# An RWKV-7 scan on one Trainium2 core: another interleaving of its steps, another order of one product, and sums over contiguous elements

## Chip, cores and metric
One core of a Trainium2 chip runs the whole program. The metric is the device time in microseconds, the median over the runs shown. The engines are named as in the profile: PE (TensorE matmul), PEld (its weight loads), DVE (VectorE), ACT (ScalarE), POOL (GpSimd) and SP (SyncE, which here issues DMAs).

## The reference, cut to what matters
Four layers on 256 latent and 256 context tokens of 1024 channels: attention, RWKV-7, pooling, attention, each followed by a squared-ReLU MLP. Only the RWKV layer's scan is touched. It runs per head (16 heads of 64), per direction, first over the context, then over the latent tokens:

```python
def step(state, inp):
    r_t, w_t, k_t, v_t, kk_t, a_t = inp
    sa = jnp.einsum("bhvk,bhk->bhv", state, kk_t)
    state = (state * w_t[:, :, None, :]
             - sa[..., None] * (kk_t * a_t)[:, :, None, :]
             + v_t[..., None] * k_t[:, :, None, :])
    return state, jnp.einsum("bhvk,bhk->bhv", state, r_t)
for d in range(N_DIRS):
    s_ctx, yc = _wkv_scan(zero, r_c, dec_c[d], key_c[d], v_c, kk_c, a_c[d], d == 1)
    _, yl = _wkv_scan(s_ctx, r_l, dec_l[d], key_l[d], v_l, kk_l, a_l[d], d == 1)
```
The output of a head is then normalised, a bonus is added, it is multiplied by a gate and projected.

## The kernel before, in words
Everything outside the scan is dense products in three matmuls of rounded parts (`mm3`, L261) and is not touched. The scan (`rwkv_scan`, L828) is written in chunks of 64 tokens. A **unit** is one pair of heads (`cc`, 8 of them) of one stream (`s`, context then latent), so there are 16 units, each with 2 directions (`dd`), 2 heads (`hh`) and 4 chunks (`q`). For a unit the kernel builds a 64 by 64 triangular matrix per chunk, inverts it, and turns the recurrence into products of 64 by 64 blocks.

The work on a unit is a set of Python generators; each `next` issues one **step**. A step is called here by its letter and number:
- **a1 to a4** (`front_a`, L920): a1 a broadcast product (L925) and DVE `kkn`; a2 eight decay products (L932) and four ACT Tanh; a3 DVE scaling and two running sums (L945), then ACT Exp `E` and `iL` and POOL `key`, `kkh`; a4 one DVE product (L960). In the order a1, a2 stand as `a`, a3, a4 as `A`.
- **b1 to b4** (`front_b`, L963): b1 four DVE and four POOL products into `KB`, `AR`; b2 and b3 sixteen PE instructions each (L978), two DVE products into `NG` (L983) and a DMA of `NG` to DRAM (`Ls`); b4 the DMA of the diagonal blocks back (`Nb`).
- **c1 to c6** (`front_c`, L990): POOL and DVE `ks`; transposes of `KB` (L1005), `AR` (L1011) and `v` (L1021) through PSUM, copied by ACT; c6 a head sum (L1028) and DVE L1029.
- **z1 to z5** (`base`, L1033): inversion of the 16 by 16 diagonal blocks on DVE, 64 blocks at once on 64 partitions. z1 to z3 eliminate inside 8 by 8 (L1049, L1051); z4 and z5 form the block off the diagonal as a product and a sum over the innermost axis of an 8 by 8 by 8 tensor (L1055 to L1059), then a transposed copy (L1060) and DMAs to DRAM (`Xs`) and back as `XT` and `X`.
- **l1 to l4** (`levels`, L1084): 16 to 32 to 64, products of 32 PE instructions (L1094) with DVE or ACT in between (L1106, L1108, L1114, L1116). **k** (`mv`, L1073): 32 more (L1078).
- **h1 to h5** (`chunks`, L1119): h1 and h2 products by the inverse (L1127), each followed by ACT copies `G` and `VU` (L1130, L1132); h3 the G products (L1137), read by DVE into `P` and `Rp` (L1143, L1144); h4 L1151; h5 L1160, read by DVE into `Q` (L1162).
- **x1 to x8** (`chain`, L1165): the state from chunk to chunk, alternately a product with DVE `S` (L1181, L1186) and an output product (L1191).
- **f1 to f3** (`finish_a`, L1196): ACT copy (L1200) and DVE add (L1201) of the output, two averages (L1204, L1208). **g** (`norms`, L1287), every fourth iteration (and one head pair at a time in the last ones): ACT table load, Ln and Exp (L1213, L1214); **G1 to G4** the DVE normalisation (L1222 to L1228), ACT and POOL (L1230, L1231); **G5, G6** the gates (L1235: PE L1237, L1238, DVE L1239, ACT L1241, DVE L1242).

The main loop (L1303) runs `n` from -4 to 15. In each turn, an **iteration**, it walks a string `STEPS`; a letter issues the next step of unit `n + AHEAD[letter]`, so units at different stages are interleaved:
```python
AHEAD = dict(l=1, k=1, x=0, z=2, c=2, f=0, h=1, b=3, a=4, g=0, G=-1, A=3, L=2)
```
From n = 0 on, PE and DVE must execute in exactly the order of the string (`ordered`, L78); ACT, POOL and the DMA queue are free to follow the framework's schedule. For n below 0 no order is forced.

PSUM has eight banks: `inv` 2, `chain` 1, `yps` 1, `pre` 2 (`pt(1)`), `lora` 1 (`pt(0)`) and `warm` 1. The last is written only by `warm`, which with `WARM = [{}]` issues none of its matmuls; it does call `later`, which places early r-projections (L883) before n = -1. SBUF tag `t1` has one buffer, shared by `kkh` and `vr`; `finish_a` works in `self.sqr`, which is also the scratch of the normalisation.

Of the kernel before, what the change touches and what calls it, by code (L numbers as in the profile page):

```python
# [6 lines left out]
F32 = mybir.dt.float32  # L7
# [13 lines left out]
class Kern:  # L21
# [806 lines left out]
    def rwkv_scan(self, R, W, U, ps, psu, K, V, Rr, hid, xr):  # L828
# [22 lines left out]
        self.it = 0  # L851
        wb = ps.tile([128, NT], F32, name="warm", tag="warm", bufs=1)
        busy = W.tile([128, T], F32R, name="busy")
        nc.scalar.copy(busy, hid["w"][:, 0:T])

# [32 lines left out]

        def warm(z):

            at = lambda plan: plan[min(self.it + 4, len(plan) - 1)].get(z, 0)
            for _ in range(at(WARM)):
                self.tc.keep_in_program_order(nc.tensor.matmul(wb[:, 0:T], lhsT=busy[:, 0:128], rhs=busy, start=True, stop=True))
            later(at(LATER))
        with self.pool("rwDram", 1, space=bass.MemoryType.DRAM) as dr:
# [21 lines left out]
            def pt(z=1):  # L917
                return ps.tile([128, NT], F32, name="pre", tag=("lora", "pre")[z], bufs=(1, 2)[z])

            def front_a(cc, s, w2, st):  # L920

                kc = K[cc]
                sl = slice(s * T, s * T + T)
                pk = pt(0)
                nc.tensor.matmul(pk[:, :T], lhsT=w2[32:64, 2], rhs=hid["kinv"][:, sl], start=True, stop=True)  # L925
                kkn = W.tile([128, T], F32, name="kkn")
                nc.vector.scalar_tensor_tensor(kkn, kc[:, sl], v["k_k"][:, cc:cc + 1], pk[:, :T], op0=ALU.mult, op1=ALU.mult)
                yield
                tw = W.tile([128, 2, T], F32, name="tw")
                ta = W.tile([128, 2, T], F32, name="ta")  # L930
                pz = [pt(dd) for dd in range(2)]
                self.in_turn([nc.tensor.matmul(pz[dd][:, z * T:z * T + T], lhsT=w2[rows(dd), z], rhs=hid[n][rows(dd), sl],  # L932
                                               start=True, stop=True) for z, n in enumerate("wa") for dd in range(2)])
                warm("a")
                for dd in range(2):
                    nc.scalar.activation(tw[:, dd], pz[dd][:, :T], AF.Tanh, bias=hb[:, dd, cc:cc + 1], scale=0.5)
                for dd in range(2):
                    nc.scalar.activation(ta[:, dd], pz[dd][:, T:], AF.Tanh, bias=hb[:, 2 + dd, cc:cc + 1], scale=0.5)
                yield

                cum = W.tile([128, 2, T], F32, name="cum")
                nc.vector.tensor_scalar(tw, tw, 1.0, -0.5 * DEC, op0=ALU.add, op1=ALU.mult)
                for dd in range(2):
                    src = tw[:, dd, ::-1] if dd else tw[:, dd]
                    nc.vector.tensor_tensor_scan(cum[:, dd], c["scanm"], src, 0.0, op0=ALU.mult, op1=ALU.add)  # L945
                E = W.tile([128, 2, 4, 65], F32, name="E")
                nc.gpsimd.memset(E[:, :, :, 0:1], 1.0)
                nc.scalar.activation(E[:, :, :, 1:65].rearrange("p d q t -> p (d q) t"),
                                     cum.rearrange("p d (q t) -> p (d q) t", q=4), AF.Exp)
                lam = W.tile([128, 2, 4], F32, name="lam", tag="lam", bufs=4)  # L950
                nc.gpsimd.tensor_copy(lam, E[:, :, :, 64])
                iL = W.tile([128, 2, T], F32, name="iL")
                nc.scalar.activation(iL, cum, AF.Exp, scale=-1.0)
                key = W.tile([128, 2, T], F32, name="key")
                nc.scalar.activation(key, ta, AF.Identity, scale=ka[:, 0, cc:cc + 1], bias=ka[:, 1, cc:cc + 1])
                nc.gpsimd.tensor_mul(key, key, kc[:, sl].unsqueeze(1).broadcast_to([128, 2, T]))
                kkh = W.tile([128, T], F32, name="kkh", tag="t1")
                nc.gpsimd.tensor_scalar_mul(kkh, kkn, 0.5)
                yield
                nc.vector.scalar_tensor_tensor(ta, ta, 1.0, kkh.unsqueeze(1).broadcast_to([128, 2, T]), op0=ALU.add, op1=ALU.mult)  # L960
                st.update(kkn=kkn, E=E, lam=lam, iL=iL, key=key, b=ta)

            def front_b(cc, s, st, it):  # L963
# [12 lines left out]
                for dd in range(2):  # L976
# [3 lines left out]
                                  for q in range(4) for hh in range(2)])  # L980
                    warm("b")
                    for hh in range(2):
# [7 lines left out]
            def front_c(cc, s, st):  # L990
# [10 lines left out]
                VU = U.tile([128, 2, 4, 2, 64], F32, name="VU", tag="VU", bufs=2)  # L1001
                for dd in range(2):
                    pn = pt().rearrange("p (q x) -> p q x", q=4)
                    for q in range(4):
                        nc.tensor.transpose(pn[:, q], flat(KB[:, dd, q]), c["ident"])  # L1005
                    warm("c")
                    nc.scalar.copy(NG[:, dd, :, :, 2], pn.rearrange("p q (h x) -> p h q x", h=2))
                    yield
                pn = pt().rearrange("p (q x) -> p q x", q=4)
                for q in range(4):  # L1010
                    nc.tensor.transpose(pn[:, q], flat(AR[:, q, 0]), c["ident"])  # L1011
                warm("d")
                nc.scalar.copy(XR[:, :, :, 0], pn.rearrange("p q (h x) -> p h q x", h=2))
                yield
                vr = W.tile([128, T], F32, name="vr", tag="t1")
# [6 lines left out]
                for dd in range(2):  # L1022
                    for par in range(2):
                        nc.scalar.copy(VU[rows(dd), dd, par::2].rearrange("p q h x -> p q (h x)"), pv[rows(par), dd])
                st.update(XR=XR, VU=VU)
                yield
                pb = pt()
# [5 lines left out]
            def base(st, it):  # L1033
# [10 lines left out]
                for j in range(7, 0, -1):  # L1044
# [6 lines left out]
                    nc.vector.tensor_sub(Z8[:, :, 0:j, j:8], Z8[:, :, 0:j, j:8], t)  # L1051
                yield
                by_row = lambda ap: ap.unsqueeze(2).broadcast_to([64, 8, 8, 8])
                by_col = lambda ap: ap.rearrange("p a b -> p b a").unsqueeze(1).broadcast_to([64, 8, 8, 8])
                nc.vector.tensor_mul(tm, by_row(N16[:, 0:8, 8:16]), by_col(Z[:, 8:16, 8:16]))  # L1055
                nc.vector.tensor_reduce(wt, tm, axis=mybir.AxisListType.X, op=ALU.add)
# [16 lines left out]
            def mv(st):  # L1073
# [3 lines left out]
                for dd, hh, q in units:  # L1077
                    nc.tensor.matmul(p[rows(g(dd)), hh, q], lhsT=NG[rows(dd), dd, hh, q, 0], rhs=VU[rows(dd), dd, q, hh],  # L1078
                                     start=True, stop=True)
                warm("k")  # L1080
                nc.scalar.copy(XR[:, :, :, 1], p)
                yield

            def levels(st):  # L1084
# [11 lines left out]
                for lv, m in enumerate((16, 32)):  # L1096
# [6 lines left out]
                    p = prod(L, of(X))  # L1103
                    warm("l")
                    if lv == 0:
# [5 lines left out]
                    if lv == 0:  # L1111
                        p2 = prod(of(XT), of(Tz))
                    warm("m")
                    nc.vector.tensor_sub(cols(XT, 1), cols(XT, 1), cols(p, 1))  # L1114
# [4 lines left out]
            def chunks(st):  # L1119
# [3 lines left out]
                for hh in range(2):  # L1123
                    p = psu.tile([128, 4, 2, 64], F32, name="inv", tag="inv", bufs=2)
                    for q in range(4):
                        for dd in range(2):
                            nc.tensor.matmul(flat(p[rows(g(dd)), q]), lhsT=XT[rows(g(dd)), hh, q],  # L1127
                                             rhs=flat(XR[rows(g(dd)), hh, q]), start=True, stop=True)
                    warm("h")
                    nc.scalar.copy(G1[:, hh], p[:, :, 0])  # L1130
                    for dd in range(2):
# [6 lines left out]
                                               rhs=flat(NG[rows(g(dd)), dd, hh, q, 1:3]), start=True, stop=True)  # L1138
                              for hh in range(2) for q in range(4) for dd in range(2)])
                warm("i")  # L1140
                for dd in range(2):
# [23 lines left out]
            def chain(st, s):  # L1165
                nonlocal S
                P, Rp, Q, yp, lam = [st[n] for n in ("P", "Rp", "Q", "yp", "lam")]
                for q in range(4):
# [7 lines left out]
                    if not (s == 0 and q == 3):  # L1176
                        bank = psu.tile([128, NT], F32, name="chain", tag="chain", bufs=1)
                        p = bank[:, 0:128].rearrange("p (d t) -> p d t", d=2)
                        for dd in range(2):
                            for hh in range(2):  # L1180
                                nc.tensor.matmul(p[rows(hh), dd], lhsT=P[rows(hh), dd, q], rhs=So[rows(hh), dd],  # L1181
                                                 start=True, stop=True)
                        warm("x")
                        S = U.tile([128, 2, 64], F32, name="S", tag="S", bufs=3)
# [11 lines left out]
            def finish_a(cc, s, yp, y2):  # L1196

                sl = slice(s * T, s * T + T)
                y = self.sqr[:, 0:T]
                nc.scalar.copy(y, yp[:, 0])  # L1200
# [33 lines left out]

            def gate(cc, w2, y):  # L1235
                pf = pt(0)
                nc.tensor.matmul(pf, lhsT=w2[:, 0], rhs=hid["g"][:, 0], start=True, stop=False)  # L1237
                nc.tensor.matmul(pf, lhsT=w2[0:32, 1], rhs=hid["g"][0:32, 1], start=False, stop=True)  # L1238
                nc.vector.tensor_mul(y, y, pf)  # L1239
                H, L = [R.tile([128, NT], F32R, name="kvr", tag="kvr", bufs=24) for _ in range(2)]  # L1240
# [46 lines left out]
            def norms(cc, s):  # L1287
# [9 lines left out]
                for c2, r in two:  # L1297
                    yield
                    gate(c2, w2s[c2][1], ycs[c2][0])
                yield  # L1300
# [36 lines left out]

AHEAD = dict(l=1, k=1, x=0, z=2, c=2, f=0, h=1, b=3, a=4, g=0, G=-1, A=3, L=2)
STEPS = [[(z, AHEAD[z]) for z in order.split()] for order in (
    "k l l l z z z z z c c c c c c h h h h h A A b b L b b a a",  # L1340
    "x x A l z x x A l z k z G l x x z G h z G h G x x c f G c G c b f c c c h f h h b L a b b a g")]

ORDERED = 0
IN_ORDER = (mybir.EngineType.PE, mybir.EngineType.DVE)

WARM = [{}]

# [158 lines left out]
```

## Time and profile before

| | us |
|---|---|
| median of 3 runs | 2518.07 |
| lowest, highest | 2516.51, 2520.76 |
| profiled execution | 2517.29 |
| its span, first to last instruction | 2515.5 |

On the page, PE is busy 93% of the span, DVE 68%, ACT 44%, POOL 13%; the granted TensorE clock of the execution is 0.963 of full speed. "PE busy" includes matmuls that wait in the array behind others. Times within the span count from its start; the scan lies between about 795 and 1345 us. An idle time in brackets behind an instruction is the engine's wait before it and what ended it. A group of matmuls is shown with the time from its first start to its last modelled end, so that the next group's start can lie before it.

### The profile page before, as it was taken

The numbers are of one execution on the slowest core, as the hardware profiler recorded it, in microseconds if no ns is written. First come the engines' busy times: TensorE is split into PE (matmuls) and PEld (weight loads), VectorE is DVE, ScalarE is ACT, GpSimd is POOL, SyncE is SP. The second block draws the span as 40 slices with busy tenths as digits, with TensorE's granted clock in tenths as the row PEclk, the third lists the DMA queues.
The fourth block names the chain that finished last, engine by engine and source line by source line (L and its number), as shares of the span: only waits on it lengthen the run. The fifth ranks groups of instructions, "written<-read, shape, count | busy, mean of one in ns | idle before, by whom it ended". The sixth has DMA issues, their size and how long they took to land.

```text
span 2515.5 us, 41677 instructions
## 1 busy us (share of the span) xinstructions
PE 2333.6 (93%) x16992; PEld 1890.5 (75%) x16992; DVE 1707.8 (68%) x2813; ACT 1102.4 (44%) x2015; POOL 325.2 (13%) x406
## 2 busy tenths in 40 slices
PE   7999999999799978878789999999999999988999
PEld 5556888888677767666667888888888888866999
DVE  5767787674786667666756777755787674787555
ACT  4678523323564334343434432323523323476443
POOL 0100001100201222222200100110001100010110
PEclk9999999999899998888989999999999999999999
DMA  7431354552123311212222355442254552203453
GB/s 279 182 112 34 126 200 175 194 200 105 69 81 98 90 37 36 40 37 37 41 60 97 118 184 214 170 168 89 80 201 170 198 199 86 73 26 109 168 185 135
DMA packets 154833, 308.32 MB, mean 123 GB/s; under 512 B 107153, under 2 KB 111633, under 8 KB 122769
## 3 DMA queue, kind: packets, MB, share of 16 engines
q1 hardware_dynamic: 154640, 305.65, 35.6%
q8 instruction: 134, 2.20, 0.4%
q14 instruction: 59, 0.48, 0.1%
HBM read 294.58 MB, written 11.03 MB: 121 GB/s over the span
## 4 chain that ended last, share of the span: by engine, by line
PE 77%; DVE 10%; ACT 5%; DMA 4%; issue 3%; POOL 1%; SPq 0%; DVEq 0%; POOLq 0%; ACTq 0%
PE mm L261 52%; PE mm L272 3%; PE po L631 2%; PE pre L261 2%; PE inv L1127 2%; DMA Nb<-Ls 1%; DMA Ls<-NG 1%; PE pre L978 1%; PE pt L626 1%; DVE wL L251 1%; PE sc L615 1%; PE rps L883 1%; ACT wH L250 1%; DVE Zb L1051 1%; PE inv L1094 1%
## 5 line engine op out<-in xcount | busy, mean ns | idle before, releaser
L251 DVE TENSOR_TENSOR wL<-wraw,wH 128x1024 fp32r<-128x1024 f32 (+1 forms) x364 | 412.1, 1135 | 268.6 <-ACT wH L250 267.7
L250 ACT CAST wH<-wraw 128x1024 fp32r<-128x1024 f32 (+1 forms) x364 | 341.9, 943 | 449.2 <-PE mm L261 430.2
L261 PE MATMUL mm<-hH,wH 128*128 128x512 f32 (+1 forms) x1296 | 471.4, 364 | 3.9 <-ACT wH L250 3.9
L261 PE MATMUL mm<-hH,wL 128*128 128x512 f32 (+1 forms) x1296 | 471.8, 364 | 1.9 <-DVE wL L251 1.8
L261 PE MATMUL mm<-hL,wH 128*128 128x512 f32 (+1 forms) x1296 | 466.6, 360 | 0.0
L261 PE MATMUL mm<-uH,wH 128*128 128x512 f32 (+1 forms) x1072 | 380.6, 355 | 0.0
L261 PE MATMUL mm<-uL,wH 128*128 128x512 f32 (+1 forms) x1072 | 379.4, 355 | 0.3
L261 PE MATMUL mm<-uH,wL 128*128 128x512 f32 (+1 forms) x1072 | 379.5, 354 | 0.0
L201 DVE SCALAR_TENSOR_TENSOR acc<-wraw,sc_sb,acc 128x2048 f32<-128x2048 f32 x126 | 302.8, 2419 | 47.9 <-DMA wraw<-in_w_mod 42.8
L392 POOL TENSOR_TENSOR usq<-relu 128x512 f32<-128x512 f32 (+1 forms) x128 | 144.8, 1132 | 1248.3 <-ACT relu L390 1248.3
L261 PEld LDWEIGHTS mm<-hH,wH 128*128 128x128 f32 x1296 | 245.5, 189 | 57.5 <-ACT wH L250 13.2
L261 PEld LDWEIGHTS mm<-hH,wL 128*128 128x128 f32 x1296 | 245.7, 190 | 42.1 <-DVE wL L251 4.4
L261 PEld LDWEIGHTS mm<-hL,wH 128*128 128x128 f32 x1296 | 245.8, 190 | 35.9 <-issue 0.2
L261 PEld LDWEIGHTS mm<-uL,wH 128*128 128x128 f32 x1072 | 202.3, 189 | 29.3 <-DVE uL L396 1.1
L261 PEld LDWEIGHTS mm<-uH,wH 128*128 128x128 f32 x1072 | 202.6, 189 | 28.3
L261 PEld LDWEIGHTS mm<-uH,wL 128*128 128x128 f32 x1072 | 202.6, 189 | 28.2
L339 DVE SCALAR_TENSOR_TENSOR x<-mm,mod,x 128x256 f32<-128x256 f32 x272 | 122.0, 479 | 133.7 <-PE mm L261 133.4
L390 ACT ACTIVATE relu<-mm 128x512 f32<-128x512 f32 (+1 forms) x128 | 69.2, 544 | 295.6 <-PE mm L261 282.8
L272 PE MATMUL mm<-hH,wH 128*128 128x256 f32 (+1 forms) x232 | 76.4, 331 | 25.9 <-ACT hH L322 14.5
L395 ACT CAST uH<-usq 128x512 fp32r<-128x512 f32 (+1 forms) x128 | 72.7, 569 | 46.4 <-POOL usq L392 46.4
L1127 PE MATMUL inv<-XR,XT 64*64 64x128 f32 x512 | 52.0, 383 | 36.7 <-DVE XT L1114 36.7
L396 DVE TENSOR_TENSOR uL<-usq,uH 128x512 fp32r<-128x512 f32 (+1 forms) x128 | 80.5, 630 | 5.6 <-ACT uH L395 4.8
(340 smaller groups left out, 3734.6 us busy)
## 6 DMA issues: line engine op xcount, KB each, us to landing
wraw<-in_w_mod SPq DMA_DIRECT2D x96, 1024.0 KB, 4.8
wraw<-in_w_in SPq DMA_DIRECT2D x64, 1024.0 KB, 6.0
wraw<-in_w_out SPq DMA_DIRECT2D x64, 1024.0 KB, 5.4
wraw<-in_w_qk SPq DMA_DIRECT2D x10, 1024.0 KB, 4.8
wraw<-in_w_rkv SPq DMA_DIRECT2D x9, 1024.0 KB, 4.8
wraw<-in_w_ao SPq DMA_DIRECT2D x16, 512.0 KB, 4.0
Ls<-NG SPq DMA_DIRECT2D x32, 128.0 KB, 2.6
XT<-Xs SPq DMA_DIRECT2D x32, 128.0 KB, 3.1
```

Source lines behind the costliest of these rows:

```text
L201: nc.vector.scalar_tensor_tensor(acc, raw, self.sc[:, k, s:s + 1], acc, op0=ALU.mult, op1=ALU.add)
L250: nc.scalar.copy(h[:, sl], raw[:, sl])
L251: nc.vector.tensor_sub(l[:, sl], raw[:, sl], h[:, sl].bitcast(F32))
L261: self.nc.tensor.matmul(ps, lhsT=a[:, k], rhs=b, start=(n == 0), stop=(n == 3 * nk - 1))
L272: self.nc.tensor.matmul(ps[:, lo:hi], lhsT=a[:, k], rhs=b, start=(k == z == 0), stop=(k == nk - 1 and z == 2))
L339: self.nc.vector.scalar_tensor_tensor(self.x[o][:, a:b], ps, G[:, o, s:s + 1], self.x[o][:, a:b], op0=ALU.mult, op1=ALU.add)
L390: nc.scalar.activation(r[:, :n], ps[:, :n], AF.Relu)
L392: nc.gpsimd.tensor_mul(u2[:, :n], r[:, :n], r[:, :n])
L395: nc.scalar.copy(uH[:, :n], u2[:, :n])
L396: nc.vector.tensor_sub(uL[:, :n], u2[:, :n], uH[:, :n].bitcast(F32))
L631: nc.tensor.matmul(po[hf * 64:hf * 64 + 64], lhsT=vn[:, k0 + kc, (2 * P + hf) * 64:(2 * P + hf) * 64 + 64], rhs=pts[hf][:, kc].rearrange(" ...
L1127: nc.tensor.matmul(flat(p[rows(g(dd)), q]), lhsT=XT[rows(g(dd)), hh, q], rhs=flat(XR[rows(g(dd)), hh, q]), start=True, stop=True)
```

## The change
It puts the steps in another order, in the string for n below 0 and in the one for n from 0 (and drops `L`, by which l1 stood at the end of the iteration before). The G products (L1137) go through the heads inside the chunks instead of outside. In z4 the off-diagonal 8 by 8 block is first copied transposed into `Zt`, and both factors of both sums are then read along contiguous elements. `v`'s transposes become c2, ahead of those of `KB` and `AR`. The bank `warm` goes and `lora` gets two buffers. `finish_a` works in a tile of tag `t1`. The gate's PSUM result is first copied to SBUF by ACT.

```diff
-        wb = ps.tile([128, NT], F32, name="warm", tag="warm", bufs=1)
-        busy = W.tile([128, T], F32R, name="busy")
-        nc.scalar.copy(busy, hid["w"][:, 0:T])
...
-        def warm(z):
+        def place(z):
             at = lambda plan: plan[min(self.it + 4, len(plan) - 1)].get(z, 0)
-            for _ in range(at(WARM)):
-                self.tc.keep_in_program_order(nc.tensor.matmul(wb[:, 0:T], lhsT=busy[:, 0:128], rhs=busy, start=True, stop=True))
             later(at(LATER))
...
-                return ps.tile([128, NT], F32, name="pre", tag=("lora", "pre")[z], bufs=(1, 2)[z])
+                return ps.tile([128, NT], F32, name="pre", tag=("lora", "pre")[z], bufs=2)
...
                 by_row = lambda ap: ap.unsqueeze(2).broadcast_to([64, 8, 8, 8])
-                by_col = lambda ap: ap.rearrange("p a b -> p b a").unsqueeze(1).broadcast_to([64, 8, 8, 8])
-                nc.vector.tensor_mul(tm, by_row(N16[:, 0:8, 8:16]), by_col(Z[:, 8:16, 8:16]))
+                by_col = lambda ap: ap.unsqueeze(1).broadcast_to([64, 8, 8, 8])
+                nc.vector.tensor_copy(Zt[:, 8:16, 8:16], Z[:, 8:16, 8:16].rearrange("p a b -> p b a"))
+                nc.vector.tensor_mul(tm, by_row(Zt[:, 8:16, 8:16]), by_col(N16[:, 0:8, 8:16]))
                 nc.vector.tensor_reduce(wt, tm, axis=mybir.AxisListType.X, op=ALU.add)
                 yield
                 nc.vector.tensor_mul(tm, by_row(Z[:, 0:8, 0:8]), by_col(wt))
...
-                              for hh in range(2) for q in range(4) for dd in range(2)])
-                warm("i")
+                              for q in range(4) for hh in range(2) for dd in range(2)])
+                place("i")
...
-                y = self.sqr[:, 0:T]
+                y = W.tile([128, T], F32, name="yf", tag="t1")
                 nc.scalar.copy(y, yp[:, 0])
...
-                nc.vector.tensor_mul(y, y, pf)
+                nc.scalar.copy(r, pf)
+                nc.vector.tensor_mul(y, y, r)
...
-AHEAD = dict(l=1, k=1, x=0, z=2, c=2, f=0, h=1, b=3, a=4, g=0, G=-1, A=3, L=2)
+AHEAD = dict(l=1, k=1, x=0, z=2, c=2, f=0, h=1, b=3, a=4, g=0, G=-1, A=3)
 STEPS = [[(z, AHEAD[z]) for z in order.split()] for order in (
-    "k l l l z z z z z c c c c c c h h h h h A A b b L b b a a",
-    "x x A l z x x A l z k z G l x x z G h z G h G x x c f G c G c b f c c c h f h h b L a b b a g")]
+    "k l l l l z z z z z c c c c c c h h h h h A A b b b b a a",
+    "G l x c c l x x c G l A k A l x x c h z G h z x x c x f G z b z c z h h h b a G G f b b f a g")]
```
The move inside `front_c` (the block of `vr`, `pv` and the `VU` copies now stands before the loop over `KB`) is left out above.

## Rows read from the trace of the kernel before

**Rows 1.** Page, part 4: the chain's shares of the span by line
```profile
PE mm L261 52%; PE mm L272 3%; PE po L631 2%; PE pre L261 2%; PE inv L1127 2%; DMA Nb<-Ls 1%; DMA Ls<-NG 1%; PE pre L978 1%; PE pt L626 1%; DVE wL L251 1%; PE sc L615 1%; PE rps L883 1%; ACT wH L250 1%; DVE Zb L1051 1%; PE inv L1094 1%
```

**Rows 2.** Windows: stretch, us; busy us (count) of PE, PEld, DVE, ACT, POOL; clock, DMA
```profile
1049.80:1078.60 28.80, 23.75 (x433) 20.53 (x432) 19.88 (x50) 10.97 (x27) 7.43 (x15) 0.88 0.24 47
...
1107.10:1147.70 40.60, 30.84 (x442) 23.11 (x442) 26.25 (x62) 18.66 (x36) 9.52 (x16) 0.83 0.25 50
```

**Rows 3.** Chain of waits, 780 to 1400 us: start us, us, what
```profile
869.63 2.50 DMA Xs<-Zb
...
877.41 1.81 PE inv L1094 x32
...
1312.93 1.08 PE inv L1094 x32
```

**Rows 4.** Timeline of PE, normal iteration: start us, us, instruction, count, idle
```profile
1045.49 1.09 PE L1005 MATMUL pre<-c_base,KB 128*128 128x128 f32 x8
...
1049.83 1.59 PE L1137 MATMUL inv<-NG,G 64*64 64x128 f32 x32
...
1052.96 1.10 PE L1160 MATMUL inv<-VU,NG 128*64 128x64 f32 x32
...
1059.79 1.15 PE L1094 MATMUL inv<-XT,Tm 64*64 64x64 f32 x32
...
1061.70 0.40 PE L1181 MATMUL chain<-S,P 64*64 64x64 f32 x8
...
1070.20 3.68 PE L1127 MATMUL inv<-XR,XT 64*64 64x128 f32 x32 [2.53 <-DVE XT L1114]
```

**Rows 5.** Windows on three short stretches, columns as in rows 2
```profile
1070.20:1073.60 3.40, 3.40 (x32) 3.40 (x34) 3.30 (x6) 1.13 (x3) 0.00 (x0) 0.50 0.02 5
...
1073.60:1075.20 1.60, 1.60 (x23) 1.48 (x20) 1.52 (x5) 1.26 (x4) 0.00 (x0) 0.50 0.00 0
...
1321.70:1323.40 1.70, 1.70 (x33) 1.70 (x34) 1.63 (x4) 0.57 (x2) 0.00 (x0) 1.00 0.00 0
```

**Rows 6.** Timeline of POOL and DVE, the same normal iteration
```profile
1064.89 1.41 POOL L971 TENSOR_TENSOR KB<-key,iL 128x256 f32<-128x256 f32 x2
...
1065.00 0.66 DVE L1051 TENSOR_TENSOR Zb<-Zb,tb 64x14 f32<-64x14 f32 x1
...
1068.51 0.18 DVE L1049 TENSOR_TENSOR tb<-Nb,Zb 64x30 f32<-64x30 f32 x1
...
1069.56 0.17 DVE L1051 TENSOR_TENSOR Zb<-Zb,tb 64x14 f32<-64x14 f32 x1
...
1075.69 0.42 DVE L970 TENSOR_TENSOR KB<-ta,iL 128x256 f32<-128x256 f32 x1
...
1076.70 0.42 DVE L972 TENSOR_TENSOR AR<-kkn,E 128x256 f32<-128x256 f32 x1
```

**Rows 7.** Groups by line, DVE, 880 to 1340 us: count, busy us, mean ns
```profile
L983 DVE TENSOR_TENSOR NG<-pre,c_rwkvB 128x512 f32<-128x512 f32 x52 | 33.5, 686 | 12.9 <-PE pre L978 12.9
...
L1058 DVE TENSOR_TENSOR tb<-Zb,tc 64x512 f32<-64x512 f32 x14 | 15.1, 1075 | 0.4
...
L1055 DVE TENSOR_TENSOR tb<-Nb,Zb 64x512 f32<-64x512 f32 x14 | 14.1, 1007 | 0.0
...
L1056 DVE TENSOR_REDUCE tc<-tb 64x64 f32<-64x512 f32 x14 | 9.5, 678 | 0.5
...
L1060 DVE COPY Zb<-Zb 64x256 f32<-64x256 f32 x14 | 5.2, 371 | 0.5
```

**Rows 8.** Timelines of ACT, PE, DVE, iteration with two gates
```profile
1109.36 0.37 ACT L1209 COPY yvar<-pre 128x256 f32<-128x256 f32 x1 [1.55 <-PE pre L1208]
...
1112.81 0.61 ACT L1214 ACTIVATE sqr<-sqr 128x512 f32<-128x512 f32 x1
...
1139.81 1.44 PE L1237 MATMUL pre<-hid_g,wg 128*128 128x512 f32 x2 [3.45 <-DVE yc L1239]
...
1140.44 0.69 DVE L1242 TENSOR_TENSOR kvr<-yc,kvr 128x512 fp32r<-128x512 f32 x1 [0.68 <-ACT kvr L1241]
```

More of the change, by code (lines that the diff above doesn't have):

```diff
@@ L933, in front_a @@
                                                start=True, stop=True) for z, n in enumerate("wa") for dd in range(2)])
-                warm("a")
+                place("a")
                 for dd in range(2):
@@ L980, in front_b @@
                                   for q in range(4) for hh in range(2)])
-                    warm("b")
+                    place("b")
                     for hh in range(2):
@@ L1001, in front_c @@
                 VU = U.tile([128, 2, 4, 2, 64], F32, name="VU", tag="VU", bufs=2)
[L1002 to L1014, printed above, removed]
                 vr = W.tile([128, T], F32, name="vr", tag="t1")
@@ L1025, in front_c @@
                 st.update(XR=XR, VU=VU)
+                yield
+                for dd in range(2):
+                    pn = pt().rearrange("p (q x) -> p q x", q=4)
+                    for q in range(4):
+                        nc.tensor.transpose(pn[:, q], flat(KB[:, dd, q]), c["ident"])
+                    place("c")
+                    nc.scalar.copy(NG[:, dd, :, :, 2], pn.rearrange("p q (h x) -> p h q x", h=2))
+                    yield
+                pn = pt().rearrange("p (q x) -> p q x", q=4)
+                for q in range(4):
+                    nc.tensor.transpose(pn[:, q], flat(AR[:, q, 0]), c["ident"])
+                place("d")
+                nc.scalar.copy(XR[:, :, :, 0], pn.rearrange("p q (h x) -> p h q x", h=2))
                 yield
@@ L1079, in mv @@
                                      start=True, stop=True)
-                warm("k")
+                place("k")
                 nc.scalar.copy(XR[:, :, :, 1], p)
@@ L1103, in levels @@
                     p = prod(L, of(X))
-                    warm("l")
+                    place("l")
                     if lv == 0:
@@ L1112, in levels @@
                         p2 = prod(of(XT), of(Tz))
-                    warm("m")
+                    place("m")
                     nc.vector.tensor_sub(cols(XT, 1), cols(XT, 1), cols(p, 1))
@@ L1128, in chunks @@
                                              rhs=flat(XR[rows(g(dd)), hh, q]), start=True, stop=True)
-                    warm("h")
+                    place("h")
                     nc.scalar.copy(G1[:, hh], p[:, :, 0])
@@ L1182, in chain @@
                                                  start=True, stop=True)
-                        warm("x")
+                        place("x")
                         S = U.tile([128, 2, 64], F32, name="S", tag="S", bufs=3)
@@ L1233, in finish_b, with gate @@
                         yield
-            def gate(cc, w2, y):
+            def gate(cc, w2, y, r):
                 pf = pt(0)
@@ L1298, in norms @@
                     yield
-                    gate(c2, w2s[c2][1], ycs[c2][0])
+                    gate(c2, w2s[c2][1], ycs[c2][0], r)
                 yield
@@ L1335 @@
 FILL = dict(mlp=[0, 0] + 24 * [1] + 6 * [0], attn=(1, 1, 2))
-AHEAD = dict(l=1, k=1, x=0, z=2, c=2, f=0, h=1, b=3, a=4, g=0, G=-1, A=3, L=2)
+AHEAD = dict(l=1, k=1, x=0, z=2, c=2, f=0, h=1, b=3, a=4, g=0, G=-1, A=3)
 STEPS = [[(z, AHEAD[z]) for z in order.split()] for order in (
-    "k l l l z z z z z c c c c c c h h h h h A A b b L b b a a",
-    "x x A l z x x A l z k z G l x x z G h z G h G x x c f G c G c b f c c c h f h h b L a b b a g")]
+    "k l l l l z z z z z c c c c c c h h h h h A A b b b b a a",
+    "G l x c c l x x c G l A k A l x x c h z G h z x x c x f G z b z c z h h h b a G G f b b f a g")]
 ORDERED = 0
 IN_ORDER = (mybir.EngineType.PE, mybir.EngineType.DVE)
-WARM = [{}]
 LATER = [dict(a=2, b=2, c=2, d=2, k=4, l=4, m=4, h=4, i=4, x=4)] * 5 + [{}]
```

## The prediction

> **What bounds the kernel now.** I read the chain of waits first, to see whether the change touches anything that counts: half of it is dense products outside the scan [rows 1], which stay. The scan enters the chain in small shares of many lines, so it is a loop in which several engines pass work round, and the question is its period. The windows on one turn give it [rows 2]: 28.8 us without gates, of which PE is busy 23.75, DVE 19.9, ACT 11.0. No engine is full; PE counts matmuls that ran slowly. A turn with two gates takes 40.6. Measured from the first product of the levels (l1) of unit 1 to that of unit 15, 14 periods take 435.5 us [rows 3]; less three gate turns at 40.6, that is 28.5 for each of the other 11. [...]
>
> **The new turn without gates, step by step.** PE and DVE must follow the new string, so I walk it from l1, in four stretches.
>
> First PE sets the pace, l1 to h2: six products of 32 narrow instructions (two take from 1059.79 to 1061.70, 1.91 us [rows 4]): 5.7. Five halves of the chain, 0.40 each with a part under the next group, taken at 0.3: 1.5. Twelve transposes at 1.09 for eight [rows 4]: 1.65. h1 and h2 at full clock 1.7 [rows 5]. Together 10.6 us. DVE's part of it is its 19.9 a turn less the third stretch (7.2) and the fourth (some 4.5), under 8.5, in short ops between products; it is covered, z1 and z2 too. If PE were quicker here, DVE would still need those 8.5.
>
> Then ACT: the copies behind one of h1 and h2 take 1.13 [rows 5]; from the end of h1 (9.75) both are done at 12.1, then f1's copy and DVE's add, 256 columns each as L970's 0.42 [rows 6]: 12.9. The ACT copy behind c5 may go first, which costs 0.6 more. I take 13.2. In the string DVE may not start z3 before this add.
>
> Then DVE alone, 7.15 us: z3, six small ops from 1068.51 to 1069.73, 1.2; b1, four ops from 1075.69 to 1077.12, 1.4 [rows 6]; z4, c6 and z5, 3.8; the first `P` and `Rp`, 256 columns each, 0.75. In z4 and z5 I price the sums anew. Both products take 1.01 and 1.08 us on 512 elements, and a plain 512-wide product 0.69 [rows 7]. The factor that steps over memory is what they have and the plain one has not, so I take 0.69 for both; the bounds are no gain at all and 0.69. The transposed copy added is bounded below by nothing but its start cost and above by L1060's 0.37 for four times the elements [rows 7]; I take 0.17. The two reductions (0.68 each) and L1060 (0.37) stay: 0.17 + 0.69 + 0.68, c6's 0.42, 0.69 + 0.68 + 0.37, and gaps, make the 3.8. Net 0.5 us a turn off DVE, with nothing to hide it: it counts in full.
>
> At 20.35 PE gets the bank for h5. It has had nothing since h4, about 6 us, because h5 needs one of the two `inv` banks and both hold G products until DVE has read them. From h5's start to the end of a2, PE and DVE alternate exactly as before: 1052.96 to 1059.79, 6.8 us [rows 4]; f2 and f3 fit into its waits. That closes the turn at 27.2 us if PE stays on its upper clock. But it waited 2.5 us before L1127 and came back at half [rows 4, 5]; after 6 us it will too. h5 and b2 stream as many columns as h1 and h2 together (32 by 64 and 16 by 128 against 32 by 128), which lost 3.4 - 1.7 = 1.7 us [rows 5]; I take 1.5 of it, as the clock may return within b2. So **28.7 us against 28.5**: the wait has moved from before h1 to before h5, and nothing is won here.
>
> Edits at nothing. The new order of the G products: they took 1.59 us [rows 4] and even a halving falls into the 6 us in which PE waits for DVE anyway; without that cover it would be worth 0.8 a turn. The diagonal blocks' round trip through DRAM, issued by SP at b3, b4, has half a turn until z1. l1 needs X, which in the first turn landed 7.8 us after z5's sums (869.63 to 877.41 [rows 3]); z5 ends near 19.6, so X is there at 27.4 and does not hold l1 at 28.7, though it would hold a turn much under 27.4. SP issues b2's and b3's DMAs behind those, and nobody needs them before the next turn's l1. The second `lora` bank, the dropped warm tile, `t1` for `finish_a` (its users are half a turn apart) and `v`'s transposes ahead of the others remove waits or add none. POOL keeps its own order; its copy for c2 now waits, through `t1`, for f3 of the turn before, which PE leaves before a2's eight products, so they and l1 hide it. Were they not there, c2 would be 0.4 late at most, as POOL's copy is 256 columns like DVE's 0.42.
>
> **A turn with gates.** DVE's work for it is 12 ops of 512 elements, 8 us, before and after. What falls is the stop in which PE waited 3.45 us for a gate's bank [rows 8]: ACT now empties it and there are two. What comes instead: G1 stands ahead of l1's DVE op, but its input comes from the table load, Ln and Exp behind f3, which now stands near the turn's end. From the copy behind f3 to the end of the last Exp is 4.06 us (1109.36 to 1113.42 [rows 8]); that copy starts some 1.2 us before l1, so both G1 ops end about 3.55 after l1's start, where l1's DVE op could have begun at 1.15: 2.4 us, in which that op, and so l2 on PE and all behind it, stands still. G2 and G3 lie partly under PE and ACT, 0.9. G4 stands in DVE's own stretch, 1.2. Each gate is DVE, ACT, DVE (0.69, 0.68 of waiting, 0.69 [rows 7, 8]) in front of b3's `NG`: 4.4 for two. Sum 8.9, against 40.6 - 28.5 = 12.1 before. So 37.6.
>
> One thing could raise this. A DVE product of two SBUF operands took 0.66 us beside POOL's product into `KB` and 0.17 without [rows 6]. [...] POOL's two additions of a gate turn now run beside z3 to z4; what they could cost is a rival below.
>
> **The sum.** 11 x 28.7 + 3 x 37.6 = 428.5, so 435.5 - 428.5 = 7 us less. The ends I take as even: the last unit's turn has no b and is shorter by 2 to 3, and the last single gate now stands behind h3 to h5, about as much later. The profiled execution took 2517.29, hence 2510.3; the median of the runs shown lies 0.8 above it, so **2511**, a gain of 0.28%.
>
> **Rivals.**
> - PE keeps its upper clock through the wait: 27.2 and 36.1, 407.5 for the 14 turns, 28 us less: **2490**. Against it stand the 0.50 of rows 5 after a shorter wait.
> - Slower, by the same wait: the lower clock holds on through b3 and a2, because PE's work between is broken by waits for `NG`. For it: 5.0 us after its return PE was still at 0.50 [rows 5]. b3 and a2 (16 by 128, 8 by 256 columns) again cost 1.7, 24 us over 14 turns: **2535**. It decides from 0.5 us a turn, where it has eaten the 7 us.
> - The change doesn't do what it says: the sums stay at 1.01 and 1.08, their price being the broadcast factors, which remain, and not the stepping. That gives back 0.71 a turn, 10 us: **2521**, no change. Against it only that the plain product has neither.
> - POOL's additions stop DVE in the gate turns: by POOL's 1.41 for two products of 256 columns [rows 6], an addition of 512 takes 1.4; two a turn on three turns, 8.4 us, **2519**, no change. Against it: only some of DVE's ops there read two SBUF operands. [...]
>
> **How the numbers follow.** Some 0.2%, 5 us, is what a measurement of this kernel can tell from no change. The forecast has 0.42; its own range is 2500 to 2515, set by f1's place behind ACT (0.3 a turn either way) and by the share of 1.7 that is lost. The upper clock 0.10, slower 0.26, sums unchanged 0.14, POOL's additions 0.08. Faster is the first two, 0.52; same the last two, 0.22; slower 0.26. The range takes in the rival at 2490, and of the slower one all but its end: 2488 to 2532.
>
> **What would show it.** Right: l1 to l1 near 28.7, PE idle some 6 us before L1160 and a granted clock of 0.50 behind it; L1127 no longer slow; L1055 and L1058 near 0.69; gate turns near 37.6, with DVE idle before L1222 for an Exp. Wrong: a period under 27.5 or over 29.3; DVE idle within z3 to z5, which I hold to be solid; L1055 still at 1.0; L1137 with PE waiting for nothing behind it, so that its new order counts.

## The result, and the profile after

The changed kernel takes **2558.8 us** (median of 4 runs, 2558.6 to 2559.0) against 2517.4 for the kernel before in the same comparison: 1.0163 times as long, 95% interval 1.0148 to 1.0177. It is slower by some 41 us, outside the predicted range. Its profiled span is 2556.9 us at a clock of 0.947, before 2515.5 at 0.963.

Turns are measured here as in the prediction, from one l1 to the next. Windows of the kernel after, columns as in [rows 2]: a turn with two gates, the end of that turn, a turn without gates, three stretches of it, and h5 to l1 of another.

```profile
998.60:1050.80 52.20, 34.15 (x442) 23.74 (x440) 29.29 (x63) 21.79 (x41) 9.16 (x14) 0.71 0.14 29
...
1034.60:1050.80 16.20, 16.20 (x56) 7.76 (x54) 6.43 (x10) 3.42 (x8) 0.83 (x3) 0.56 0.24 58
...
1081.40:1111.70 30.30, 24.66 (x434) 20.39 (x433) 19.32 (x51) 10.78 (x26) 6.62 (x12) 0.83 0.21 41
...
1096.10:1101.56 5.46, 0.00 (x0) 0.03 (x1) 5.32 (x14) 0.00 (x0) 0.12 (x1) 0.86 0.00 0
...
1101.56:1110.20 8.64, 8.64 (x69) 6.77 (x70) 3.20 (x7) 0.65 (x2) 0.43 (x2) 0.50 0.48 91
...
1110.40:1111.70 1.30, 1.30 (x11) 0.69 (x9) 0.77 (x2) 0.37 (x1) 0.40 (x1) 1.00 0.00 0
...
1216.20:1224.10 7.90, 7.90 (x80) 6.21 (x80) 4.14 (x8) 1.02 (x3) 1.13 (x4) 0.79 0.54 102
```

The turn without gates is 30.3 us (28.8 in [rows 2], forecast 28.7), the one with gates 52.2 (40.6, forecast 37.6). From 1096.10 on PE does nothing for 5.46 us while DVE is busy; from 1101.56 on it is busy for all of 8.64 us, at a granted clock of 0.50; only then does the clock return. PE's timeline of the same turn, to set against [rows 4]:

```profile
1081.35 1.15 PE L1091 MATMUL inv<-X,NG 64*64 64x64 f32 x32
...
1089.90 1.96 PE L1124 MATMUL inv<-XR,XT 64*64 64x128 f32 x32
...
1093.86 1.10 PE L1134 MATMUL inv<-NG,G 64*64 64x128 f32 x32
...
1094.89 1.15 PE L1148 MATMUL yps<-NG,VU 128*64 128x64 f32 x32
...
1101.56 1.98 PE L1157 MATMUL inv<-VU,NG 128*64 128x64 f32 x32 [5.52 <-DVE Rp L1141]
...
1103.47 2.08 PE L973 MATMUL pre<-AR,KB 64*128 64x128 f32 x16
```

The wait stands where it was forecast: h5 starts 20.2 us after l1 (20.35 forecast). h1 and h2 take 1.96 us instead of 3.68, the G products 1.10 instead of 1.59. But h5 and b2 (L973) take nearly twice what they take at 1.00 (1.15 and 1.16 us in fill_chain, below). DVE's products of z4 and z5, against [rows 7]:

```profile
L1052 DVE TENSOR_TENSOR tb<-Zb,Nb 64x512 f32<-64x512 f32 x13 | 8.9, 683 | 0.4
...
L1055 DVE TENSOR_TENSOR tb<-Zb,tc 64x512 f32<-64x512 f32 x13 | 8.8, 673 | 0.0
```

They fell from 1007 and 1075 ns to 683 and 673. Now the turn with gates: timelines of ACT, PE, DVE and POOL, to set against [rows 8].

```profile
997.56 0.37 ACT L1206 COPY yvar<-pre 128x256 f32<-128x256 f32 x1 [2.51 <-PE pre L1205]
...
997.95 1.28 ACT L106 ACT_TABLE_LOAD   x1
...
999.24 1.28 ACT L931 ACT_TABLE_LOAD   x1
...
1002.12 1.28 ACT L1210 ACT_TABLE_LOAD   x1
...
1004.76 1.28 ACT L1211 ACT_TABLE_LOAD   x1
...
1006.59 0.61 ACT L1211 ACTIVATE sqr<-sqr 128x512 f32<-128x512 f32 x1
...
1008.40 1.97 PE L1091 MATMUL inv<-XT,Tm 64*64 64x64 f32 x32 [8.08 <-DVE Tm L1103]
...
1032.70 1.97 PE L1157 MATMUL inv<-VU,NG 128*64 128x64 f32 x32 [8.99 <-DVE Rp L1141]
...
1037.76 2.08 PE L1234 MATMUL pre<-hid_g,wg 128*128 128x512 f32 x2
...
1024.06 1.27 DVE L1044 TENSOR_TENSOR tb<-Nb,Zb 64x24 f32<-64x24 f32 x1
...
1024.03 2.48 POOL L1228 TENSOR_TENSOR yc<-yc,kvr 128x512 f32<-128x512 f32 x2 [2.29 <-ACT yc L1227]
```

Between the copy behind f3 and the last Exp, ACT now loads tables four times and does a2's Tanh: 9.6 us instead of 4.06. PE stands 8.08 us before l2, 8.99 before h5, and then makes the gates' products at the lower clock (0.56 over the second window above).

Over the whole scan, from the first products of l1 in the timelines ("normal" is the mean of 10 turns in us, "gate" of 3; the last turn and the ends stand outside). The turns are those of the one profiled execution, which was the slowest of ten for fill_and_g and gorder_only and the fastest of ten for sums_only:

| kernel | median, us | ratio to before, 95% | normal | gate |
|---|---|---|---|---|
| before | | | 28.1 | 40.9 |
| after | 2558.8 | 1.0163 [1.0148, 1.0177] | 30.2 | 50.4 |
| lora_one | 2592.6 | 1.0303 [1.0283, 1.0324] | 33.2 | 50.3 |
| fill_wait | 2574.3 | 1.0228 [1.0203, 1.0253] | 30.4 | 50.8 |
| inv_three | 2560.5 | 1.0172 [1.0147, 1.0197] | 30.3 | 49.9 |
| g_before_a | 2534.2 | 1.0070 [1.0050, 1.0091] | 30.1 | 42.9 |
| fill_chain | 2536.5 | 1.0081 [1.0066, 1.0096] | 27.6 | 48.3 |
| fill_and_g | 2515.5 | 0.9990 [0.9977, 1.0004] | 27.6 | 44.4 |
| old_steps_sqr | 2502.5 | 0.9940 [0.9919, 0.9961] | 27.9 | 38.8 |
| sums_only | 2515.8 | 0.9988 [0.9978, 0.9999] | 28.2 | 40.7 |
| gorder_only | 2509.4 | 0.9971 [0.9956, 0.9985] | 28.0 | 40.1 |
| parts_best | 2492.5 | 0.9911 [0.9894, 0.9927] | 27.4 | 36.1 |
| order_one | 2527.5 | 1.0036 [1.0025, 1.0047] | 29.0 | 43.9 |
| order_five | 2467.8 | 0.9809 [0.9795, 0.9824] | 24.8 | 37.5 |

In each comparison the ratio is to the kernel before on the same chip, whose median was between 2515.5 and 2519.3. In the two profiled spans, 41.4 us apart, the normal turns make 10 x 2.03 = 20 and the gate turns 3 x 9.5 = 28; the ends give back 7 (the last turn takes 26.6 instead of 31.2, what follows the last l1 is 3.3 shorter, the first l1 0.6 later).

### The profile page after: what moved, and what is told of

Read it like the earlier page. It is cut to its first block, busy times and chain, and to the rows that moved or that the text cites. A ratio compares the mean times of both kernels' runs of the same rounds, so it can differ in the third digit from the quotient of the medians.

```text
span 2556.9 us, 41760 instructions
## 1 busy us (share of the span) xinstructions
PE 2352.1 (92%) x16992; PEld 1894.3 (74%) x16992; DVE 1709.5 (67%) x2829; ACT 1114.3 (44%) x2028; POOL 322.3 (13%) x406
## 5 line engine op out<-in xcount | busy, mean ns | idle before, releaser
L1157 PE MATMUL inv<-VU,NG 128*64 128x64 f32 x512 | 29.1, 299 | 82.7 <-DVE Rp L1141 82.7
L1157 PEld LDWEIGHTS inv<-VU,NG 128*64 128x64 f32 x512 | 26.7, 208 | 84.7 <-issue 84.5
```

The costliest lines, as they stand in the source:

```text
L1157: nc.tensor.matmul(p[rows(hh), dd, q], lhsT=NG[:, dd, hh, q, 2], rhs=VU[:, dd, q, hh], start=True, stop=True)
```

## The experiments

**lora_one, fill_wait, inv_three.** The first only goes back to one bank; the others use the bank so freed.

```diff
-                return ps.tile([128, NT], F32, name="pre", tag=("lora", "pre")[z], bufs=2)
+                return ps.tile([128, NT], F32, name="pre", tag=("lora", "pre")[z], bufs=(1, 2)[z])
```

> The kernel after with one `lora` bank, as before; one PSUM bank is left idle. It is the measure for the next two, which need that bank. Theory A (the added time is PE's lower clock behind its wait before h5, plus the gate turns): only the second gate product has to wait for the first one's copy out, about 1 us in each of 3 gate turns, so 2559 to 2563 us. Theory B (some other product used the second bank in every turn): over 0.5 us in each of 14 turns, 2566 or more.

34 us slower than after: theory B. PE's timeline from h5 to l1 shows two new waits, f2 for a1's bank and a2 for f3's:

```profile
1243.85 1.22 PE L1201 MATMUL pre<-yf,c_rwkvB 128*128 128x256 f32 x2 [0.62 <-DVE kkn L922]
...
1248.70 1.22 PE L927 MATMUL pre<-hid_w,wl 64*128 64x256 f32 x4 [0.46 <-ACT yvar L1206]
```

The new order puts a1, f2, f3 and a2, which all use these banks, into one stretch. The two waits make 1.1 of the 3.1 us by which a normal turn is longer; in the turn shown PE's products also stay slow for longer: the next l1 takes 1.97 us instead of 1.15. The second bank is no spare: without it the new order loses nearly twice as much.

fill_wait adds to it, in h4's step (the tiles `wb`, in the idle bank, and `busy` are made ahead of the scan, as in the kernel before):

```diff
+    for _ in range(36):
+        nc.tensor.matmul(wb[:, 0:T], lhsT=busy[:, 0:128], rhs=busy, start=True, stop=True)
```

> As lora_one, and behind h4 PE runs 36 products into the idle bank whose result nobody reads (128 x 128 by 256 columns; at 0.117 us each, half of the 0.23 of the 512-wide ones, about 4.2 us), so that the 5.5 us in which PE waits for Rp are mostly filled. Theory A, the clock: PE stays at 1.00 from h5 to a2, that stretch falls from 10.1 to about 8.3 us in the 10 turns without gates, and somewhat in the gate turns: 15 to 22 us less than lora_one, about 2542. Theory B, the waits: from h5 to a2 PE waits for DVE's NG at each product and the clock is only a by-product: within 4 us of lora_one, or slower.

18 us less than lora_one, as theory A has it, but one bank's waits still lie in the stretch in question. So it was done again without them (fill_chain, below).

inv_three adds to lora_one `tag="inv", bufs=3` in place of 2.

> As lora_one, with a third `inv` bank, so that h5 needs not wait until DVE has read P and Rp. Both theories expect h5 right behind h4, about 1.1 us at full clock, and no wait for Rp. Theory A: PE's next wait is then 1 to 2 us for b1 and the rest behind b2 for NG; h5 and b2 leave the slow stretch, turns without gates fall from 30.3 to about 27.5, bounded by the landing of X: 2515 to 2530. Theory B (the order of DVE's work sets the turn, whichever PE product stands behind it): only h5 leaves it, 1.9 us a turn, and PE comes back as slow as before: 2535 or more.

32 us less than lora_one. The time is theory B's; the gain of a normal turn, 2.9 us, is more than its 1.9. PE's timeline: h5 follows h4 at once and takes 1.10 us, and the wait has moved to the next products that need DVE.

```profile
1240.47 1.10 PE L1157 MATMUL inv<-VU,NG 128*64 128x64 f32 x32
...
1243.69 1.40 PE L973 MATMUL pre<-AR,KB 64*128 64x128 f32 x14 [1.71 <-DVE kvr L1024]
...
1248.91 1.22 PE L1201 MATMUL pre<-yf,c_rwkvB 128*128 128x256 f32 x2 [2.67 <-DVE kkn L922]
```

b2 waits for the bank that DVE's c6 must free, f2 for DVE's `kkn`; together 4.4 us of waiting, and b3 again takes 2.08. Freeing one product from DVE's stretch does not keep PE working through it.

**fill_chain: the clock alone.** fill_wait's 36 products, with both `lora` banks, into a tile of the `chain` bank. They are issued in all 16 units.

> The kernel after, both `lora` banks kept, and behind h4 36 products of 256 columns (4.57 us in fill_wait) whose result nobody reads, into the `chain` bank, which is free by then. This is the clock alone: no wait of the kernel after is changed. Theory A: h5 falls from 1.98 to 1.15 us, b2 from 2.08 to 1.16, and the stretch from h5 to l1 from 10.1 to 10.5 to about 7.8; 10 turns without gates give back 2.4 each, the gate turns a little: 20 to 30 us under the kernel after, 2529 to 2539. Theory B (the waits for DVE in that stretch are what is slow): 2554 to 2560.

Theory A, to the size: 22 us under the kernel after. PE's timeline, then the windows of the filled wait and of h5 to the next l1:

```profile
1087.14 4.58 PE L1155 MATMUL chain<-busy 128*128 128x256 f32 x36
...
1092.73 1.15 PE L1162 MATMUL inv<-VU,NG 128*64 128x64 f32 x32 [1.01 <-DVE Rp L1143]
...
1093.81 1.16 PE L975 MATMUL pre<-AR,KB 64*128 64x128 f32 x16
...
1099.36 1.15 PE L1093 MATMUL inv<-X,NG 64*64 64x64 f32 x32
```

```profile
1087.10:1092.70 5.60, 4.62 (x40) 4.38 (x36) 5.46 (x14) 0.00 (x0) 0.12 (x1) 1.00 0.01 3
...
1092.70:1099.40 6.70, 6.54 (x80) 4.86 (x80) 4.20 (x8) 1.19 (x4) 0.83 (x3) 1.00 0.64 120
```

The end of the wait has not moved (h4's start to h5's is 6.7 us in both), no wait was taken away, and the same products take 6.6 us at 1.00 instead of 10.1: h5 1.15, b2 1.16. In the profiled spans the 14 turns are 30 us shorter and the ends 5.5 longer. Work that nobody reads makes this kernel faster.

**g_before_a: the late Exp.**

```diff
-    ... h h h b a G G f b b f a g"
+    ... h h h b a G G f b b f g a"
```

> The kernel after, with the two last letters of the order exchanged: the norms' table load, Ln and Exp come ahead of a2's Tanh. Theory A: the 8 us in which DVE waits for Exp between l1 and l2 of a gate turn come from ACT's loading four tables, because a2's Tanh stand between the early load and Ln; now one load serves Ln and Exp, they end some 4 us after f3's copy, l1 to l2 falls from 9.8 to 4 to 5 us: 15 to 18 us less over three gate turns, 2541 to 2544. Theory B (Exp is late because f3 is late): the wait stays over 7 us, 2555 to 2560.

Theory A, though with 25 us under after where it had 15 to 18. ACT's and PE's timelines:

```profile
1132.36 0.37 ACT L1206 COPY yvar<-pre 128x256 f32<-128x256 f32 x1 [2.51 <-PE pre L1205]
...
1132.75 1.28 ACT L106 ACT_TABLE_LOAD   x1
...
1135.80 0.61 ACT L1211 ACTIVATE sqr<-sqr 128x512 f32<-128x512 f32 x1
...
1136.43 1.28 ACT L931 ACT_TABLE_LOAD   x1
...
1137.61 1.15 PE L1091 MATMUL inv<-XT,Tm 64*64 64x64 f32 x32 [2.56 <-DVE Tm L1103]
```

One load serves Ln and Exp, which end 4.05 us from the copy's start; Tanh's load comes after. PE's wait before l2 is 2.56 instead of 8.08, in three turns 17 us. The three gate turns together are 22.5 shorter; nearly all of the other 6 lies at the end of the second, where h5 to l1 took 13.5 us instead of 19.3. That part was not isolated.

**fill_and_g.** Both edits.

> fill_chain and g_before_a in one kernel. Theory A (the lower clock and the late Exp are two causes that add up, and together they are more than the loss): 22 and 25 us under the kernel after, 2508 to 2516, at or a little below the kernel before. Theory B (they share a part, since the gate turns lose by both): 2520 to 2532.

Theory A, at the upper end of its range: level with before. By the ratios, after's 1.63% fell by 0.82 with the fill, by 0.93 with the letters, and by 1.73 with both. The two causes add up, and are the whole loss against the kernel before. Against the same edits in the old order (the next run) some 0.5% stays, which no run took apart.

**The edits without the order.** old_steps_sqr is the kernel after with the strings and `AHEAD` of before and `y = self.sqr[:, 0:T]`. The gate's copy also writes that tile, so that `y` is not kept in this run; parts_best, below, gives it a tile of its own.

> Everything of the change but the order of the steps (the two strings and the `AHEAD` line are those of before, and `finish_a` works in its old tile, as the old order needs). Theory A (all that was lost lies in the order): the sums save 0.5 us a turn, the G products up to 0.5, the stop of 3.45 us for a gate's bank in 3 turns is gone: faster than before, 2498 to 2512 us, so that the order alone costs 45 to 60. Theory B (another edit costs too, such as v's copy on POOL or the gate's copy on ACT): 2520 or more.

Theory A: 0.6% faster than before. All that was lost, and 0.6% more, lies in the order and the tile that it needs for `y`.

> The kernel before with the new sums alone. Theory A: the two products fall from 1.01 and 1.08 to about 0.69 each, the copy adds 0.2, and since PE waits for DVE before h1 the 0.5 us a turn count in full: 5 to 9 us less, 2509 to 2513. Theory B (PE's wait before h1 is set by something else, and the gain is lost in another wait): 2515 to 2520.

Only 3 us, theory B, though both products fell as far as forecast (groups by line, then DVE's wait for the blocks' way through DRAM):

```profile
L1056 DVE TENSOR_TENSOR tb<-Zb,Nb 64x512 f32<-64x512 f32 x14 | 9.6, 683 | 0.5
...
L1059 DVE TENSOR_TENSOR tb<-Zb,tc 64x512 f32<-64x512 f32 x14 | 9.5, 681 | 0.4
...
DVE tb L1049 <- DMA Nb<-Ls: 28.2, 13, 4.8
```

The wait of z1 for `Nb` is about that of the kernel before (us in total, times, longest), whose two rows follow (the G products over 14 units, and that wait):

```profile
L1137 PE MATMUL inv<-NG,G 64*64 64x128 f32 x448 | 22.7, 278 | 0.0
...
DVE tb L1049 <- DMA Nb<-Ls: 27.6, 12, 5.8
```

In the old order DVE runs into that DMA 12 times, and a shorter z does not bring it forward. That this is where the rest went is read from the wait alone; it was not isolated.

> The kernel before with the G products' new order alone (heads inside the chunks). Theory A: they take 1.10 instead of 1.59 us, as in the kernel after, and since DVE waits for them before P, 0.3 to 0.5 us a turn: 4 to 8 us less, 2510 to 2514. Theory B, the prediction's price of nothing also without the cover: 2515 to 2520.

Theory A, 0.29% or 7 us. The G products by line:

```profile
L1137 PE MATMUL inv<-NG,G 64*64 64x128 f32 x448 | 15.5, 276 | 0.0
```

15.5 us instead of 22.7 for the same 448 instructions, each of which takes as long as before (276 and 278 ns). More of them run side by side: by their start times in the traces, they start in pairs, some 6 ns apart, in the kernel before (from 1049.83 on, mostly 0.11 us from pair to pair in each half of the list), and with the new list in fours (kernel after, from 1093.86 on, 0.11 us from four to four). In the old list a pair differs in its input rows (`dd`) and the output rows (`hh`) stay the same for 16 products; in the new one they change every second product, so that four neighbours use every pair of input and output rows once.

parts_best has the new sums, the new order of the G products, the gate's copy by ACT and two `lora` banks in the kernel before, with `y = W.tile([128, T], F32, name="yf", tag="yf")`.

> The kernel before, its order and its transposes' order kept, with the new sums, the new order of the G products, the gate's copy by ACT, two `lora` banks, and a tile of its own for `finish_a`. Theory A (the order is the whole loss, the other edits are gains that add up: 3.5, 10 and some 4 to 9 for the gates): 2497 to 2506, faster than both kernels. Theory B (v's transposes ahead of the others, which this one leaves out, carried part of the gain seen in old_steps_sqr): 2507 to 2515.

Faster than both kernels, 5 us under theory A's range, and by the ratios 0.3% faster than old_steps_sqr, from which the order of the transposes and the tile of `y` set it apart; which of the two it was, no run tells. Theory B's gain from moving v's transposes is not there.

**Another order.** The kernel after with

```diff
-    "G l x c c l x x c G l A k A l x x c h z G h z x x c x f G z b z c z h h h b a G G f b b f a g"
+    "l x c c A l x x c l k A G z l x x c G h z h G x x c x c z z f z h h G b h b a G G f b b f g a"   (order_one)
+    "l x c c A l x x c l k A G z l x x c G h z h z G x x c x z f c z h h G b a h b G G f b f b g a"   (order_five)
```

> The kernel after in a third order of the steps: a3 moves up into DVE's wait between l1 and l2, z1 to before l4, z4 and z5 to before f1's neighbours so that P and Rp come early, b1 behind them (under h5), norms before a2, and G1 to G4 apart from one another behind l3. Theory A (the wait before h5 and the lower clock behind it, and the late Exp, are the whole loss): PE's wait before h5 falls from 5.5 us to under 2.5, a turn without gates to 25 to 27.5 us, a gate turn to 34 to 38: 2465 to 2495. Theory B (X's way through DRAM, 7.8 us from the end of z5, or DVE's sum of 20 us and its waits set the turn): 28.5 or more a turn, 2510 or more.

Theory B by its size: 29.0 us a normal turn. The wait before h5 fell to 0.5 to 1.3 us, but others came. Timelines of PE and DVE:

```profile
1082.81 1.15 PE L1148 MATMUL yps<-NG,VU 128*64 128x64 f32 x32 [2.91 <-DVE yf L1198]
...
1106.80 0.42 DVE L1024 SCALAR_TENSOR_TENSOR kvr<-pre,kvr 128x256 f32<-128x256 f32 x1 [2.84 <-PE pre L1023]
```

h4 writes the `yps` bank, which f1's add must first have read, and that stood behind z4; DVE's c6 waited for a head sum at the end of PE's queue.

> As order_one, mended where its trace showed new waits: z3 stands behind h2, f1 ahead of c6 and z5 (h4 waited 2.9 us for f1's add, DVE's c6 up to 2.8 us for its head sum), b1 and a1 go under h5, the gates behind b2, f2 and f3 behind them. Theory A (with the wait before h5 under 2 us PE keeps its upper clock and the turn falls to what DVE needs): 25 to 27 us a turn without gates, 35 to 38 with, 2465 to 2500. Theory B (X's way through DRAM behind z5, or waits between DVE and PE that the order only moves, hold the turn): 28 or more, 2515 or more.

Theory A: **1.9% faster than before**, some 90 us under the kernel after. PE's timeline, a window of 24.3 us, and PE's wait for X over the scan (us in total, times, longest):

```profile
1057.01 1.15 PE L1157 MATMUL inv<-VU,NG 128*64 128x64 f32 x32 [0.92 <-DVE Rp L1141]
...
1058.34 1.16 PE L973 MATMUL pre<-AR,KB 64*128 64x128 f32 x16 [0.18 <-DVE AR L967]
...
1060.79 1.66 PE L973 MATMUL pre<-AR,KB 64*128 64x128 f32 x16 [0.66 <-DVE NG L978]
...
1065.00:1089.30 24.30, 20.88 (x419) 17.18 (x416) 20.73 (x51) 11.59 (x27) 7.74 (x13) 1.00 0.24 43
...
PE inv L1091 <- DMA X<-Xs: 4.8, 6, 1.4
```

PE waits 0.92 us before h5, 0.18 before b2 and 0.66 before b3. The window lies in the next turn, which takes 25.2 us from l1 to l1: the clock is 1.00 throughout, and DVE is busy for 20.7 of its 24.3 us. The normal turns take 24.3 to 25.8; before l1 PE now waits for X to land 6 times, so that a part of theory B's wait is there.

## Why the prediction was wrong

- **Stretches one to three** were right: h5 at 20.2 us against 20.35, the sums at 0.68 against 0.69, PE's wait 5.5 against some 6.
- **Stretch four failed**: "I take 1.5 of it, as the clock may return within b2". From h5 to l1 it was 10.1 us, not 8.3; the clock came back behind b3, and until then products took nearly double (h5 1.98 us, b2 2.08, a1 1.22; in fill_chain 1.15, 1.16 and 0.69). That is the slower rival (2535) by its size, 1.7 a turn where 1.8 was measured, but not by its reason: it had PE's work broken by waits for `NG`, and PE was busy for all of the 8.64 us. The half clock's length had been taken from the 5.0 us of [rows 5]. Eight of the ten normal turns are like the one shown (10.1 to 10.5 us from h5 to l1); in the other two the same wait of 5.5 us was followed by 7.9 and 8.2 us, about the forecast (the window from 1216.20 on, mean clock 0.79). What sets that length was not isolated. That the clock is the cause, fill_chain shows: with PE kept at 1.00, h5 to l1 took 6.6 us, where the prediction had 6.8, and a normal turn 27.6, where the rival of the upper clock had 27.2.
- **The gate turn failed at its first term**: "From the copy behind f3 to the end of the last Exp is 4.06 us". That row is of a turn in which nothing else was on ACT in that stretch. In the new string a2 stands between f3 and g, and its Tanh went between the early table load and Ln. The wait was 8.08, not 2.4. With the letters exchanged it was 2.56, so the term was right for an order that the change doesn't have. In g_before_a a single load of 1.28 us (1132.75) serves Ln and Exp; in the kernel after, with Tanh in between, Ln and Exp each have a load of their own (1002.12 and 1004.76, 1.28 us each).
- **Its other terms** (the turn shown against the normal one shown): the wait for Exp made l1 to l2 longer by 8.1 us, against 2.4. The gates were priced by DVE and ACT, 4.4 us for two (the durations named add up to 4.1). PE bound them: four groups of products from 1037.76 on, 8.0 us at a granted clock of 0.50. G2 and G3 (l2 to h4) cost 2.3 against 0.9. G4 with z3 (h4 to h5) cost 3.5 against 1.2: two small DVE ops beside POOL's addition took 1.27 and 1.18 us instead of 0.18 and 0.17 (the same two in the turn without gates, from 1095.03). That is the POOL rival, 2.1 us a turn instead of 2.8; read from the rows, no run took it away. Both read two SBUF operands, and they ended at 1025.33 and 1026.55, POOL's two additions at 1025.30 and 1026.51. A DVE op with an operand in PSUM, L1114 of the kernel before, took 0.40 us both beside POOL's `key` product (1062.37) and without POOL (1069.65). In sum 21.9 over a normal turn, forecast 8.9.
- **Edits at nothing**: the G products' order lies ahead of a wait of 5.5 us and should be worth nothing there, as forecast, though no run took it out of the kernel after; in the old order it is worth 7 us, 0.5 a turn, where the prediction had 0.8 without that cover. The second `lora` bank was named as removing waits; that the new order depends on it (34 us) was not seen.
- **The ends** were not even: with the last turn they are 7 us shorter, to the good.
- **X's landing**, at 27.4 us, was said to hold only a turn much under that. It holds no turn of the kernel after; where turns are shorter PE does wait for it before l1: 6 times in order_five, 4.8 us in all.

Against the 428.5 us forecast for 14 turns, 479.7 were measured: 14.7 more in ten normal turns, 38.5 in the gate turns, 2.1 less in the last.

## What to carry to other kernels

When an order is changed, walk every engine's queue through it, not only those whose order is forced: a duration between two rows holds only as long as nothing new stands between them, as a2's Tanh and the table loads around it did here (9.6 us instead of 4.06). A wait of 5.5 us on PE cost twice here, the second time by some 3.5 us on what followed it at the lower clock: price that tail by the rival's full length, or fill the wait (fill_chain) or shorten it (order_five, under 1 us in the turn shown). Test each part of a change alone; here the part that was meant as the main one hid gains of 0.9% in the others, and another order turned the same edits into 1.9%.

## What the runs showed of the hardware

- In the kernel after, after a wait of 5.5 us PE stayed at 0.50 for 8.6 us in which the profile shows it busy throughout (8.64 of 8.64 us, from 1101.56); in two of ten such turns the clock came back earlier (mean 0.79 from 1216.20 to 1224.10, 0.76 from 898.10 to 906.30). In fill_chain, with 36 products of 128 by 128 by 256 in the wait (4.58 us), it was 1.00 from the wait to l1.
- The same 32 products of 64 by 64 by 128 took 1.59 us in the old order (kernel before) and 1.10 in the new (kernel after), in which four neighbours use all four pairs of input and output rows; their start times show fours there and pairs in the old one. Over 14 units they were 22.7 us in the kernel before and 15.5 in gorder_only, which changes the order alone.
- With Tanh between the early table load and Ln (kernel after) ACT made four table loads of 1.28 us between 997.95 and 1006.04, with Tanh behind Exp (g_before_a) two between 1132.75 and 1137.71, the first for Ln and Exp together.
